# The third pooled group on VectorE, and one written order from the attention splits to the last output weights

## The chip, the cores and the metric

The kernel runs on one core of a Trainium2 chip. The metric is the device time of one launch in microseconds (us); less is better. The engines of the core run beside one another and wait for each other through semaphores: TensorE (PE in the profile; its weight loads are PEld), VectorE (DVE), ScalarE (ACT), GpSimd (POOL) and SyncE (SP), which here only issues transfers. Each engine takes its own instructions strictly in the order in which they stand.

## The reference

One layer of a streaming encoder for 1024 tokens of width 1024 (`D_MODEL`). The change lies in the first third, the mixer; the gated feed-forward, the embedding gate and the last norm follow unchanged. Of the columns of `z` the first 512 are pooled; the rest are queries, keys and values.

```python
h = x
hn = rmsnorm(h, norm_mix_g[i])
z = hn @ w_in[i]
u = z[..., :POOL_W]
q, k, v = jnp.split(z[..., POOL_W:], 3, axis=-1)
a = pool_mixer(u, pool_w[i], pool_b[i], pool_scale[i])
o = chunk_attention(q, k, v, rel_bias[i])
h = h + jnp.concatenate([a, o], axis=-1) @ w_out[i]
...
```

`pool_mixer` takes four groups of 128 channels with trailing windows of 2, 4, 8 and 16 tokens. For each group it forms the mean over the window, subtracts the token itself, multiplies by a 128x128 matrix of the group, adds a bias and scales:

```python
for gi, win in enumerate((2, 4, 8, 16)):
    start = jnp.maximum(t + 1 - win, 0)
    cnt = (t + 1 - start).astype(jnp.float32)
    pooled.append((cs[:, t + 1, gi] - cs[:, start, gi]) / cnt[None, :, None])
y = jnp.stack(pooled, axis=2) - ug
y = jnp.einsum('bsgc,gcd->bsgd', y, w) + b.reshape(N_POOL, POOL_GROUP)
return y.reshape(B, S, POOL_W) * scale
```

## The kernel before

Channels lie on the 128 partitions and tokens run along the free dimension, in two halves of 512. Every product keeps nearly fp32 precision: each operand is split into a high part, which ScalarE copies (`hi`, L122), and a low part, which VectorE forms as source minus `hi` (`lo`, L123), and `mm3` (L117 to L119) makes three matmuls, hi·hi, hi·lo and lo·hi. So one split is one ScalarE instruction and then one VectorE instruction, and a matmul of the second kind waits for the `lo`.

The mixer runs in units: for pairs of heads TensorE makes scores, transposed probabilities and values, and in the gaps it fills in the input projection of the next columns. The generator `rest()` holds these projections; the last four are the pooled groups, in the order 2, 3, 0, 1. When group g is projected, VectorE moves it from PSUM to the tile U (L555), and `project_u` appends the window sums of the group to the list `later`. Each group is done in four quarters of 256 tokens: for a window of 4 there are two additions with shifted operands (L568, 271 and 269 columns), a multiplication by 1/window (L580) and a subtraction (L581), and in the quarter with the first tokens two short instructions more (L578, L579), since their windows are shorter. All of it runs on GpSimd, `LATER` = 8 entries after each unit, and what is left runs after the last projection (`run_later(len(later))`).

Then comes the output projection of the first token half. Its first pass over eight column blocks takes the attention rows of `w_out`, `out_mm(d, 0, ..., attn, ...)`: 4 x 3 matmuls per block, each block in its own PSUM bank (2, 3, 4, 5, 0, 1, 6, 7 in turn). After blocks 2 to 5 of this pass it runs `mix(g)` for groups 2, 3, 0, 1: a split of the group (`yh`, `yl`, 1024 columns), six matmuls with the group's matrix into banks 6 and 7, two ScalarE evacuations with bias and scale into `a32` (L592), and splits of these into `catp`, the pooled rows of the next operand. All mixes use banks 6 and 7, so that the matmuls of one wait for the evacuations of the mix before. The second pass takes the pooled rows into the same eight banks, VectorE adds each bank to the residual H (L772), and the second token half follows, which also needs `cat_o(1)`, the split attention output of that half.

`out_weights(n, cs)` loads four pieces of `w_out` into a ring of four raw buffers (L601) and splits them (`[128, 4, 128]` pieces, 512 columns, which the profile counts as 128x512). H is loaded from `xT` into room that the attention output, U and `a32` held (L764).

The order of TensorE is written out for the whole kernel (`manual_schedule`). That of ScalarE and VectorE is written out for the units and, in a second block, up to the split of the mix matrices (`pwh`, `pwl`). What follows that block, the mixes among it, is placed by a list scheduler, with `cat_o(1)` at a raised priority. SyncE and GpSimd are placed by the scheduler throughout.

## Time and profile before

| | us |
|---|---|
| median of 3 runs | 1138.48 |
| their range | 1138.35 to 1140.33 |
| profiled execution | 1138.08 |
| its span | 1136.1 |
| TensorE busy | 1118.4 |
| VectorE busy | 858.9 |
| ScalarE busy | 586.4 |
| GpSimd busy | 183.6 |

The profiled execution is one more run, 0.40 us under the median. The span goes from its first to its last instruction; 1.98 us lie around it. In the rows a tile stands by its name: R and B are the split operands, F holds fp32 data, PS is PSUM. `out<-in` gives what an instruction writes and reads, a line number is that of the kernel shown, "idle before" is how long the engine stood still before the instruction, and the name after the arrow is what ended that. A row with x4 joins four instructions that followed on one another, and its time is that of all four.

### The profile page before, as it was taken

The numbers are of one execution on the slowest core, as the hardware profiler recorded it, in microseconds if no ns is written. First come the engines' busy times: TensorE is split into PE (matmuls) and PEld (weight loads), VectorE is DVE, ScalarE is ACT, GpSimd is POOL, SyncE is SP. The second block draws the span as 40 slices with busy tenths as digits, with TensorE's granted clock in tenths as the row PEclk, the third lists the DMA queues.
The fourth block names the chain that finished last, engine by engine and source line by source line (L and its number), as shares of the span: only waits on it lengthen the run. The fifth ranks groups of instructions, "written<-read, shape, count | busy, mean of one in ns | idle before, by whom it ended". The sixth has DMA issues, their size and how long they took to land.

```text
span 1136.1 us, 16167 instructions
## 1 busy us (share of the span) xinstructions
PE 1118.4 (98%) x5914; PEld 935.1 (82%) x5914; DVE 858.9 (76%) x1442; ACT 586.4 (52%) x1020; POOL 183.6 (16%) x230
## 2 busy tenths in 40 slices
PE   9999999999799999999999999999999999999997
PEld 7988898888688888888888888888888888888887
DVE  7566766778658888887787788777878889986845
ACT  8376766664654554444444444444444445574634
POOL 0010001088402210120112010301030102000000
PEclk9999999999999999999999999999999999999999
DMA  7111110115500154585557655765576556520003
GB/s 278 38 38 43 38 43 23 56 56 161 173 12 17 49 149 146 131 176 148 134 147 162 164 144 143 165 165 130 150 160 158 144 149 126 153 93 19 1 31 118
DMA packets 64879, 125.91 MB, mean 111 GB/s; under 512 B 7328, under 2 KB 8736, under 8 KB 64800
## 3 DMA queue, kind: packets, MB, share of 16 engines
q1 hardware_dynamic: 50688, 99.38, 27.0%
q0 software_dynamic: 13824, 25.17, 13.9%
q8 instruction: 46, 0.75, 0.3%
q10 hardware_dynamic: 288, 0.33, 0.1%
q14 instruction: 33, 0.27, 0.1%
HBM read 110.18 MB, written 14.68 MB: 110 GB/s over the span
## 4 chain that ended last, share of the span: by engine, by line
PE 90%; POOL 4%; DVE 2%; issue 2%; ACT 1%; DMA 0%; SPq 0%; POOLq 0%; DVEq 0%; ACTq 0%
PE PS L117 28%; PE PS L118 28%; PE PS L119 28%; POOL F L568 2%; PE PS L382 2%; PE PS L447 1%; PE PS L405 1%; PE PS L448 1%; POOL F L581 1%; POOL F L580 1%; DVE B L425 1%; DMA F<-in_xT 0%; DVE F L350 0%; PE PS L744 0%; ACT F L362 0%
## 5 line engine op out<-in xcount | busy, mean ns | idle before, releaser
L117 PE MATMUL PS<-R 128*128 128x512 f32 (+1 forms) x1104 | 425.4, 385 | 0.7 <-DVE F L453 0.6
L118 PE MATMUL PS<-R 128*128 128x512 f32 (+1 forms) x1104 | 422.0, 382 | 0.3 <-DVE R L227 0.3
L119 PE MATMUL PS<-R 128*128 128x512 f32 (+1 forms) x1104 | 421.6, 382 | 0.0
L117 PEld LDWEIGHTS PS<-R 128*128 128x128 f32 x1104 | 207.9, 188 | 44.6 <-issue 2.3
L118 PEld LDWEIGHTS PS<-R 128*128 128x128 f32 x1104 | 207.8, 188 | 41.1 <-DVE R L227 1.4
L119 PEld LDWEIGHTS PS<-R 128*128 128x128 f32 x1104 | 207.6, 188 | 40.3
L122 ACT ACTIVATE R<-F 128x512 fp32r<-128x512 f32 (+2 forms) x221 | 137.7, 637 | 181.0 <-PE PS L118 84.4
L123 DVE TENSOR_TENSOR R<-F,R 128x512 fp32r<-128x512 f32 (+2 forms) x221 | 160.1, 740 | 41.3 <-ACT R L122 38.8
L1135 DVE TENSOR_TENSOR F<-F,PS 128x512 f32<-128x512 f32 x140 | 92.8, 682 | 6.2 <-PE PS L119 6.0
L122 ACT ACTIVATE BQ<-RW 128x512 fp32r<-128x512 f32 x90 | 52.6, 623 | 82.0 <-PE PS L118 78.0
L825 DVE TENSOR_TENSOR F<-F 128x512 f32<-128x512 f32 x88 | 61.8, 702 | 42.5 <-DMA F<-in_w_up 41.6
L1078 POOL DMA_DIRECT2D RW<-Yd x56 | 49.6, 887 | 257.9 <-DMA RW<-Yd 200.8
L1078 POOL DMA_DIRECT2D RW<-in_w_down x40 | 36.1, 943 | 234.4 <-DMA RW<-in_w_down 192.2
L123 DVE TENSOR_TENSOR BQ<-RW,BQ 128x512 fp32r<-128x512 f32 x90 | 59.2, 687 | 2.9 <-PE PS L118 2.1
L118 PE MATMUL PS<-BQ 128*128 128x512 f32 x140 | 54.6, 390 | 0.1
L117 PE MATMUL PS<-R,BQ 128*128 128x512 f32 x140 | 54.5, 389 | 0.0
L119 PE MATMUL PS<-BQ 128*128 128x512 f32 x140 | 54.5, 389 | 0.0
L119 PE MATMUL PS<-R,BQ 128*128 128x512 f32 x140 | 54.5, 389 | 0.0
L117 PE MATMUL PS<-BQ 128*128 128x512 f32 x140 | 54.5, 389 | 0.0
L118 PE MATMUL PS<-R,BQ 128*128 128x512 f32 x140 | 54.5, 389 | 0.0
L362 ACT ACTIVATE F<-F,small 128x640 f32<-128x640 f32 (+4 forms) x64 | 44.0, 688 | 15.2 <-DVE small L350 13.5
L961 ACT ACTIVATE F<-F,vec 128x1024 f32<-128x1024 f32 (+1 forms) x25 | 28.6, 1143 | 43.6 <-DVE F L936 37.5
(177 smaller groups left out, 1726.2 us busy)
## 6 DMA issues: line engine op xcount, KB each, us to landing
F<-in_w_up SPq DMA_DIRECT2D x91, 256.0 KB, 3.9
RW<-Yd SPq DMA_DIRECT2D x60, 256.0 KB, 3.7
RW<-Yd POOLq DMA_DIRECT2D x56, 256.0 KB, 5.3
RW<-in_w_down SPq DMA_DIRECT2D x50, 256.0 KB, 2.9
RW<-in_w_down POOLq DMA_DIRECT2D x40, 256.0 KB, 6.0
Yd<-F SPq DMA_DIRECT2D x40, 256.0 KB, 3.7
F<-in_w_in SPq DMA_DIRECT2D x10, 512.0 KB, 3.5
F<-in_xT SPq DMA_DIRECT2D x16, 256.0 KB, 5.8
```

Source lines behind the costliest of these rows:

```text
L117: pe.matmul(ps, ahi, bhi, start=first, stop=False, skip_group_check=more)
L118: pe.matmul(ps, ahi, blo, start=False, stop=False, skip_group_check=more)
L119: pe.matmul(ps, alo, bhi, start=False, stop=last, skip_group_check=more)
L122: both = (act.activation(hi, src, AF.Copy), dve.tensor_tensor(lo, src, rv(hi), ALU.subtract))
L123: dve.tensor_tensor(lo, src, rv(hi), ALU.subtract))
L362: push(1.9 + 0.85 * z, lambda S=S, s_=s_: act.activation(S, S, AF.Exp, bias=s_[:, 0:1], scale=-1.0, accum_out=s_[:, 1:2]))
L382: pe.matmul(PS[:, places[x][y], 0:wide], q[halves[x], t * P:(t + 1) * P], k[halves[x], ki + y * wide:ki + (y + 1) * wide], start=i == 0, s ...
L568: pool.tensor_tensor(d, x, y, ALU.add))
L825: return dve.tensor_tensor(rawu[to], rawu[a], rawu[b], op)
L961: act.activation(y, Gb[:, 2 + a:2 + b], AF.Identity, bias=vec[:, C_CB + fi:C_CB + fi + 1], scale=cw(2))
L1078: pool.dma_start(t, src, accum_op=ALU.add)
L1135: dve.tensor_tensor(t, t, PS[:, 4 + d], ALU.subtract if n in (1, 5) else ALU.add)
```

## The change

Group 1, which is projected last, has its window sums on VectorE. They go to a list of their own, `tail`, and use two buffers of their own, `temps`. Multiplication and subtraction are one instruction there (`scalar_tensor_tensor`, L586 of the changed kernel), so that a quarter has three instructions in place of four, 14 for the group in place of 18.

The written order of ScalarE and VectorE reaches further: the second `manual_schedule` block now ends after the splits of the pooled output weights and `cat_o(1)`. The split of a pooled group is a function of its own, `pooled_split`, and stands apart from `mix`; the operand buffers `ya` are laid out per group. In `mix` both evacuations come ahead of both splits, and `mix(3)` calls `pooled_split(1)` in between. `run_later(len(later))` is called ahead of the block.

```diff
+        temps = [f(57.5, 272), f(58.5625, 272)]
...
-        later = []
+        later, tail = [], []
...
-            Ta, Tb = T1, T2
+            Ta, Tb = (T1, T2) if g != 1 else temps
+            eng, queue = (pool, later) if g != 1 else (dve, tail)
             for q in (3, 2, 1, 0):
...
-                    later.append(lambda d=dst[:, lo_:n], x=src[:, lo_:n], y=src[:, lo_ - m:n - m]:
-                                 pool.tensor_tensor(d, x, y, ALU.add))
+                    queue.append(lambda d=dst[:, lo_:n], x=src[:, lo_:n], y=src[:, lo_ - m:n - m]:
+                                 eng.tensor_tensor(d, x, y, ALU.add))
...
-        def pool_out(g, q, u, src):
+                queue.append(lambda q=q, u=u, src=src: pool_out(g, q, u, src, eng))
+
+        def pool_out(g, q, u, src, eng):
...
-            pool.tensor_tensor(src[:, f0:n], src[:, f0:n], cnt[:, win - 1:win].to_broadcast([P, n - f0]), ALU.mult)
-            pool.tensor_tensor(u[:, f0:n], src[:, f0:n], u[:, f0:n], ALU.subtract)
-
-        def mix(g):
-            yh, yl = ya[g % 2]
+                eng.tensor_tensor(src[:, HIST:f0], src[:, HIST:f0], cnt[:, 0:win], ALU.mult)
+                eng.tensor_tensor(u[:, HIST:f0], src[:, HIST:f0], u[:, HIST:f0], ALU.subtract)
+            if eng is pool:
+                eng.tensor_tensor(src[:, f0:n], src[:, f0:n], cnt[:, win - 1:win].to_broadcast([P, n - f0]), ALU.mult)
+                eng.tensor_tensor(u[:, f0:n], src[:, f0:n], u[:, f0:n], ALU.subtract)
+            else:
+                eng.scalar_tensor_tensor(u[:, f0:n], src[:, f0:n], 1.0 / win, u[:, f0:n], ALU.mult, ALU.subtract)
+
+        def pooled_split(g):
+            split(U[:, g, HIST:], *ya[g])
+
+        def mix(g, between=None):
+            yh, yl = ya[g]
             a32 = a32s[g % 2]
-            split(U[:, g, HIST:], yh, yl)
             for h in range(2):
...
                 act.activation(a32[:, hs], ps, AF.Identity, bias=pbs[:, g:g + 1],
                                scale=vec[:, C_PS + g:C_PS + g + 1])
+            if between:
+                between()
+            for h in range(2):
+                hs = slice(h * 512, (h + 1) * 512)
                 split(a32[:, hs], catp[h][:, g, 0], catp[h][:, g, 1])
...
-        ya = [(r(144 + 8 * s, 1024), r(148 + 8 * s, 1024)) for s in range(2)]
+        ya = {g: (r(b, 1024), r(b + 4, 1024)) for g, b in ((2, 144), (3, 152), (0, 136), (1, 144))}
...
+        run_later(len(later))
         with tc.manual_schedule(engines={mybir.EngineType.Activation, mybir.EngineType.DVE}):
             out_weights(1, attn)
             cat_o(0)
+            pooled_split(2)
             for _ in fill:
                 flush()
             flush()
             split(pw, pwh, pwl)
-        run_later(len(later))
-        with tc.high_priority(AHEAD):
+            pooled_split(3)
+            out_weights(0, attn)
+            for fn in tail[:6]:
+                fn()
+            pooled_split(0)
+            for fn in tail[6:]:
+                fn()
+            for z, d in enumerate(first_d):
+                out_mm(d, 0, first_b[z], attn, True, False)
+                if 1 <= z <= 4:
+                    mix((2, 3, 0, 1)[z - 1], (lambda: pooled_split(1)) if z == 2 else None)
+            out_weights(1, pooled)
+            out_weights(0, pooled)
             cat_o(1)
...
-        out_weights(0, attn)
-        first_b = (2, 3, 4, 5, 0, 1, 6, 7)
-        for z, d in enumerate(first_d):
-            out_mm(d, 0, first_b[z], attn, True, False)
-            if 1 <= z <= 4:
-                mix((2, 3, 0, 1)[z - 1])
         for d in first_d:
             sp.dma_start(H[d], xT[d])
-        out_weights(1, pooled)
-        out_weights(0, pooled)
```

The order of TensorE's instructions is the same before and after. On GpSimd the 18 instructions of group 1 are gone and the rest stands as it was. The other three engines differ at the following places.

VectorE from the last projection to the first residual addition. Before, L555 is the evacuation of the last projection, `B<-F,B` with 1024 columns the `lo` of a pooled group, `R<-F,R` with 4x128 a piece of `w_out`, and with 512 a piece of the attention output or of a mix:

```order
L555 TENSOR_TENSOR F<-PS,F 128x512
L123 TENSOR_TENSOR B<-F,B 128x512
L123 TENSOR_TENSOR R<-F,R 128x4x128 x4
L123 TENSOR_TENSOR B<-F,B 128x1024
L123 TENSOR_TENSOR R<-F,R 128x4x128 x2
L123 TENSOR_TENSOR R<-F,R 128x512
L123 TENSOR_TENSOR B<-F,B 128x1024
L123 TENSOR_TENSOR R<-F,R 128x512
L123 TENSOR_TENSOR R<-F,R 128x4x128
```

After, the end of the window sums of group 1 (the first rows; three quarters of three instructions each and the `lo` of group 0 stand ahead of them) and what follows on it:

```order
L570 TENSOR_TENSOR F<-F 128x271
L570 TENSOR_TENSOR F<-F 128x269
L580 TENSOR_TENSOR F<-F,small 128x4
L581 TENSOR_TENSOR F<-F 128x4
L586 SCALAR_TENSOR_TENSOR F<-F 128x252
L123 TENSOR_TENSOR R<-F,R 128x512 x2
L123 TENSOR_TENSOR B<-F,B 128x1024
L123 TENSOR_TENSOR R<-F,R 128x512 x6
L123 TENSOR_TENSOR R<-F,R 128x4x128 x8
L123 TENSOR_TENSOR R<-F,R 128x512 x4
```

Before, the pooled pieces of `w_out` (4x128) stand scattered between the mixes; after, all eight follow the last mix, and the four pieces of `cat_o(1)` (the last row), which stood ahead of the last projection's evacuation, close the block.

ScalarE at the mixes, before (L592 is an evacuation of a mix, the rows with L122 are `hi` copies):

```order
L122 ACTIVATE R<-F 128x4x128 x5
L592 ACTIVATE F<-PS,small,vec 128x512
L122 ACTIVATE R<-F 128x4x128
L122 ACTIVATE R<-F 128x512
L592 ACTIVATE F<-PS,small,vec 128x512
L122 ACTIVATE B<-F 128x1024
L122 ACTIVATE R<-F 128x512
L122 ACTIVATE R<-F 128x4x128
```

and after, where L599 is that evacuation:

```order
L122 ACTIVATE R<-F 128x4x128 x4
L122 ACTIVATE B<-F 128x1024
L599 ACTIVATE F<-PS,small,vec 128x512 x2
L122 ACTIVATE R<-F 128x512 x2
L599 ACTIVATE F<-PS,small,vec 128x512 x2
L122 ACTIVATE B<-F 128x1024
L122 ACTIVATE R<-F 128x512 x2
L599 ACTIVATE F<-PS,small,vec 128x512 x2
```

The fifth piece of weights, the first of the pooled rows, no longer stands ahead of the first evacuation, and the `hi` of group 1 (the last row with 1024 columns) stands between the evacuations of `mix(3)` and its splits.

SyncE's transfers, before (`in_w_out` are the output weights, `in_xT` the residual, `in_w_up` the first weights of the feed-forward):

```order
L764 DMA F<-in_xT 128x1024 x4
L601 DMA F<-in_w_out 128x512 x6
L764 DMA F<-in_xT 128x1024
L601 DMA F<-in_w_out 128x512
L821 DMA F<-in_w_up 128x512 x2
L601 DMA F<-in_w_out 128x512
L764 DMA F<-in_xT 128x1024
L821 DMA F<-in_w_up 128x512 x4
L764 DMA F<-in_xT 128x1024
```

and after (L783, L612 and L838 are the same three):

```order
L783 DMA F<-in_xT 128x1024
L612 DMA F<-in_w_out 128x512 x4
L838 DMA F<-in_w_up 128x512 x2
L783 DMA F<-in_xT 128x1024 x2
L612 DMA F<-in_w_out 128x512 x4
L838 DMA F<-in_w_up 128x512 x4
L783 DMA F<-in_xT 128x1024 x4
```

Four of the residual's loads, those of blocks 4 to 7, moved from the front to the end, behind all output weights and six loads for the feed-forward: their room is that of the attention output, which `cat_o(1)` now reads last.

More of the change, by code (lines that the diff above doesn't have):

```diff
@@ L566, in project_u @@
                     lo_ += m
-                    later.append(lambda d=dst[:, lo_:n], x=src[:, lo_:n], y=src[:, lo_ - m:n - m]:
-                                 pool.tensor_tensor(d, x, y, ALU.add))
+                    queue.append(lambda d=dst[:, lo_:n], x=src[:, lo_:n], y=src[:, lo_ - m:n - m]:
+                                 eng.tensor_tensor(d, x, y, ALU.add))
                     src, dst = dst, (Tb if dst is Ta else Ta)
                     m *= 2
-                later.append(lambda q=q, u=u, src=src: pool_out(g, q, u, src))
-        def pool_out(g, q, u, src):
+                queue.append(lambda q=q, u=u, src=src: pool_out(g, q, u, src, eng))
+        def pool_out(g, q, u, src, eng):
             win, n, f0 = WINDOWS[g], HIST + 256, HIST
@@ L577, in pool_out @@
                 f0 = HIST + win
-                pool.tensor_tensor(src[:, HIST:f0], src[:, HIST:f0], cnt[:, 0:win], ALU.mult)
-                pool.tensor_tensor(u[:, HIST:f0], src[:, HIST:f0], u[:, HIST:f0], ALU.subtract)
-            pool.tensor_tensor(src[:, f0:n], src[:, f0:n], cnt[:, win - 1:win].to_broadcast([P, n - f0]), ALU.mult)
-            pool.tensor_tensor(u[:, f0:n], src[:, f0:n], u[:, f0:n], ALU.subtract)
-        def mix(g):
-            yh, yl = ya[g % 2]
+                eng.tensor_tensor(src[:, HIST:f0], src[:, HIST:f0], cnt[:, 0:win], ALU.mult)
[9 more added lines that the diff above has]
+            yh, yl = ya[g]
             a32 = a32s[g % 2]
-            split(U[:, g, HIST:], yh, yl)
             for h in range(2):
@@ L696, in cat_o @@
                 split(o32[:, c, h * 512:(h + 1) * 512], cato[h][:, c, 0], cato[h][:, c, 1])
+        first_d = (4, 5, 6, 7, 0, 1, 2, 3)
+        first_b = (2, 3, 4, 5, 0, 1, 6, 7)
+        run_later(len(later))
         with tc.manual_schedule(engines={mybir.EngineType.Activation, mybir.EngineType.DVE}):
@@ L754, in rows @@
                     act.activation(dst, self.out, AF.Copy)
-        first_d = (4, 5, 6, 7, 0, 1, 2, 3)
-        out_weights(0, attn)
-        first_b = (2, 3, 4, 5, 0, 1, 6, 7)
-        for z, d in enumerate(first_d):
-            out_mm(d, 0, first_b[z], attn, True, False)
-            if 1 <= z <= 4:
-                mix((2, 3, 0, 1)[z - 1])
         for d in first_d:
             sp.dma_start(H[d], xT[d])
-        out_weights(1, pooled)
-        out_weights(0, pooled)
         tc.keep_in_program_order(act.activation(small[:, 2:3], mhalf, AF.Gelu))
```

## The prediction

> **What bounds the kernel now.** I read the page first, then the busy time by stage, then TensorE's own rows and waits where the stage has a hole.

> ```profile
> PE 1118.4 (98%) x5914; PEld 935.1 (82%) x5914; DVE 858.9 (76%) x1442; ACT 586.4 (52%) x1020; POOL 183.6 (16%) x230
> PE 90%; POOL 4%; DVE 2%; issue 2%; ACT 1%; DMA 0%; SPq 0%; POOLq 0%; DVEq 0%; ACTq 0%
> 0.00:263.00 263.00, 258.66 (x2016) 221.66 (x2017) 176.50 (x415) 171.77 (x347) 48.26 (x84) 1.00 0.21 69
> 263.00:310.50 47.50, 41.24 (x179) 32.54 (x178) 37.84 (x42) 27.78 (x46) 30.65 (x35) 0.96 0.59 186
> 310.50:1136.00 825.50, 818.52 (x3723) 680.88 (x3722) 644.52 (x985) 386.85 (x627) 104.70 (x112) 1.00 0.47 120
> ```

> The stage rows give length, then busy time of PE, PEld, DVE, ACT and POOL, granted clock, DMA share. TensorE is the bound everywhere; 47.5 us around the mixes hold 6.3 us of its idle time and a clock of 0.96. GpSimd's 4% of the chain lie there too. TensorE's order does not change, so a gain can only be its waits and its slow clock there.

> ```profile
> 273.99 0.39 PE L117 MATMUL PS<-R 128*128 128x512 f32 x1
> 285.17 0.50 PE L117 MATMUL PS<-B 128*128 128x512 f32 x1 [1.10 <-ACT F L592]
> 285.93 0.50 PE L118 MATMUL PS<-B 128*128 128x512 f32 x1 [0.26 <-DVE B L123]
> 287.04 0.50 PE L117 MATMUL PS<-B 128*128 128x512 f32 x1 [0.37 <-ACT F L592]
> 299.39 0.80 PE L117 MATMUL PS<-B 128*128 128x512 f32 x1 [4.52 <-ACT F L592]
> 302.81 0.39 PE L119 MATMUL PS<-R 128*128 128x512 f32 x1
> 310.56 0.39 PE L117 MATMUL PS<-R 128*128 128x512 f32 x1
> 295.00:300.00 5.00, 0.60 (x2) 0.51 (x3) 1.81 (x2) 2.90 (x5) 1.99 (x5) 0.92 0.18 68
> 300.00:305.00 5.00, 5.00 (x18) 3.98 (x17) 4.29 (x8) 4.98 (x10) 0.00 (x0) 0.74 0.67 224
> ```

> At 273.99 the first attention pass of the output projection begins, at 310.56 the pooled pass. Between them stand 8 x 12 matmuls and four mixes of 6, 120 in all. From 302.81 to 310.56 there are 34 starts in 7.75 us, 0.228 each; 120 would take 27.4 us and they take 36.57. So **9.2 us** are lost: about 2.3 around `mix(3)` (285 to 287), 4.7 ahead of `mix(1)`, and most of the rest after it, where the clock fell for a while ((0.08 + 0.26) x 5 = 1.7 us).

> Why TensorE waits:

> ```profile
> 283.82 0.63 ACT L122 ACTIVATE R<-F 128x512 fp32r<-128x512 f32 x1 [7.92 <-DMA F<-in_w_out]
> 284.36 0.76 ACT L592 ACTIVATE F<-PS,small,vec 128x512 f32<-128x512 f32 x1
> 276.42 1.18 POOL L581 TENSOR_TENSOR F<-F 128x254 f32<-128x254 f32 x1
> 279.61 0.95 POOL L568 TENSOR_TENSOR F<-F 128x271 f32<-128x271 f32 x1 [2.00 <-DVE F L555]
> 296.36 0.71 POOL L581 TENSOR_TENSOR F<-F 128x252 f32<-128x252 f32 x1
> ACT B L122 <- POOL F L581: 5.7, 1, 5.7
> 277.04 0.69 DVE L555 TENSOR_TENSOR F<-PS,F 128x512 f32<-128x512 f32 x1
> 279.98 4.24 DVE L123 TENSOR_TENSOR R<-F,R 128x512 fp32r<-128x512 f32 x4
> 284.14 1.74 DVE L123 TENSOR_TENSOR B<-F,B 128x1024 fp32r<-128x1024 f32 x1
> 298.19 1.22 DVE L123 TENSOR_TENSOR B<-F,B 128x1024 fp32r<-128x1024 f32 x1 [3.27 <-ACT B L122]
> 300.56 3.10 DVE L123 TENSOR_TENSOR R<-F,R 128x512 fp32r<-128x512 f32 x5 [0.55 <-ACT R L122]
> ```

> First, ScalarE stood 7.9 us at a piece of the pooled weights that had not landed, with the first evacuation of `mix(2)` queued behind it; `mix(3)` waited for that bank. Second, GpSimd began group 1 at 279.61 and ended at 297.07; ScalarE's split of the group stood 5.7 us for it, and `mix(1)` with it. The last rows show what both engines cost each other: a `lo` of 512 columns takes 1.06 us while GpSimd runs (4.24 for four) and 0.62 when it rests (3.10 for five); one of 1024 takes 1.74 against 1.22.

> **The change, part by part.** *Group 1 on GpSimd* goes: 17.5 us from 279.61 to 297.07, and with it VectorE's slow rate after group 0 ends at 277.60.

> *Group 1 on VectorE.* No row shows it; the nearest are

> ```profile
> 1114.73 0.43 DVE L1285 TENSOR_TENSOR F<-V,F 128x256 f32<-128x256 f32 x1 [0.88 <-ACT F L1284]
> 1115.19 0.42 DVE L1286 TENSOR_TENSOR F<-F 128x256 f32<-128x256 f32 x1
> L978 DVE SCALAR_TENSOR_TENSOR F<-F,V 128x512 f32<-128x512 f32 x20 | 13.8, 688 | 0.0
> L1286 DVE TENSOR_TENSOR F<-F 128x512 f32<-128x512 f32 x13 | 8.9, 689 | 0.2
> L617 DVE TENSOR_TENSOR small<-vec 128x4 f32<-128x4 f32 x1 | 0.2, 164 | 1.8 <-DMA vec<-in_vecs 1.8
> ```

> Two additions of 256 columns, the second needing the first, start 0.46 apart; 15 columns more make 0.47. The fused form costs as much as an addition (688 against 689 at 512), so 0.46. Eight additions, four fused, two short ones of 0.20: 3.76 + 1.84 + 0.40 = **6.0 us**. The upper bound is the rate beside GpSimd, 1.06, so 14.8; the lower the bare durations, 5.5. I take 6.0, since GpSimd is idle by then.

> [...]

> *Is that in time for `mix(1)`?* TensorE's 273.99 rests on `cat_o(0)`, which moves ahead there, so I keep it. With no waits TensorE reaches `mix(1)` after 78 matmuls, at 291.8, its second half at 292.5. VectorE's written order:

> ```profile
> 264.48 0.63 ACT L122 ACTIVATE R<-F 128x512 fp32r<-128x512 f32 x1 [3.66 <-DMA F<-in_w_out]
> 268.60 0.85 DVE L453 TENSOR_TENSOR F<-PS,F 64x256 f32<-64x256 f32 x2
> L592 ACT ACTIVATE F<-PS,small,vec 128x512 f32<-128x512 f32 x8 | 5.9, 765 | 0.0
> L122 ACT ACTIVATE B<-F 128x1024 fp32r<-128x1024 f32 x4 | 4.2, 1047 | 5.7 <-POOL F L581 5.7
> 266.87 4.28 ACT L122 ACTIVATE R<-F 128x512 fp32r<-128x512 f32 x8
> ```

> - The first `lo` can start when its `hi` ends, 265.1. Eight splits beside GpSimd 8.5, two value additions 0.85, the `lo` of group 2 1.66, some 0.3 for the second weight piece to land: 276.4.
> - Two evacuations and the mix matrices, 3 x 0.61: 278.2. Group 3, 1.14: 279.4 (`mix(3)` needs it at 283.6). Four attention weights, 2.4: 281.8 (needed at 289.0).
> - Six steps of the chain 2.8, the `lo` of group 0 1.14, eight steps 3.2: 289.0. Two splits of `mix(2)` 1.2, the `lo` of group 1 1.2: 291.4, just ahead of 291.8.

> ScalarE stands at the `hi` of group 1 until 289.0, and queued behind it are the splits of `mix(3)` and the evacuations of `mix(0)`, for which `mix(1)` waits: 1.0 + 2 x 0.53 (4.28 for eight) + 0.77 = 2.8, so bank 6 is free at 291.8 and bank 7 at 292.4. Both paths end within 0.4 us of TensorE. From here each us that the chain is late costs TensorE a us. I allow **0.3 us** for hops between engines.

> *Pooled weights after the last mix.* ScalarE no longer stands at their transfers with an evacuation behind it, which removes the waits at `mix(3)`. The first four now end near 299.3: `mix(1)` ends at 293.2, its evacuations, splits and four `hi` take 1.5 + 1.1 + 2.1, and VectorE trails by one piece. Needed at 301.4; hidden with 2 us. The second four wait for their ring slots, land some 3 us after, and are split near 304; needed four blocks later, at 312.3.

> *`cat_o(1)` last.* It ends on VectorE near 307; nobody needs it before the second token half, 8 x 12 matmuls after 301.4, at 323.2. Early on, three `hi` copies of 0.6 us leave ScalarE between 161 and 215, where TensorE hardly waits (4.3 us idle in the 263 of the first stage row): 0 to 0.9 us, taken as nothing.

> *SyncE.* The loads of H for blocks 4 to 7 go past the pooled weights and six feed-forward loads, and wait for `cat_o(1)`:

> ```profile
> 273.81 2.95 SPq L764 DMA_DIRECT2D F<-in_xT  x4
> DMA to landing us min/median/max: 3.4/3.9/5.7
> 313.48 0.69 DVE L772 TENSOR_TENSOR F<-F,PS 128x512 f32<-128x512 f32 x1 [4.26 <-PE PS L119]
> ```

> Issued from about 305 to 307 instead of 273.8 to 276.8, with 3.4 to 5.7 to land, they come between 309 and 313. VectorE's first residual addition, at 313.48 before, could start at 304.1 and waits for them then, with the other additions queued behind it. TensorE only notices at 323.2, when it takes the first bank again: cover of some 9 us, and no cost.

> *Sum.* 9.2 - 0.3 = 8.9 us. Against the profiled execution, 1138.08 - 8.9 = 1129.2; the median of the runs lies 0.4 higher, so **1129.6 us**. With the whole 9.2 and the 0.9 of the early copies, 1128.4.

> **The rivals.** *The mixes wait for VectorE in part (1131 to 1134).* If the two engines shut each other out for whole instructions, each split beside GpSimd would take its own 0.69 and all of a GpSimd addition, 0.64 alone:

> ```profile
> 264.28 0.64 POOL L568 TENSOR_TENSOR F<-F 128x271 f32<-128x271 f32 x1
> ```

> That is 1.33 in place of 1.06; eight of them make the chain 2.2 us late, and `mix(1)` with it: 1131.8. For it: the slow rows are real. Against: four took 4.24, not 5.3. [...] Any other delay of VectorE counts alike; steps of 0.7 in place of 0.46 would cost 3.4, so 1133.0. And a wait as long as the old one would bring the slow clock back, 1.7 us more.

> *No change.* ScalarE, whose order is now fixed, passes the stall on: if the chain ended at 297 as GpSimd did, `mix(1)` would start at 299.8, and all would be as before, 1138. It would need steps of 1.0 us on an engine without a neighbour; the rows speak against it.

> *Slower: the residual's loads.* If H for blocks 4 to 7 landed so late that VectorE's additions did not free the first bank by 323.2, TensorE would stand at the second half. The last load may land up to 321 or so, 14 us after its issue; from there each us costs one, and past 23 us the gain is gone: landing after 28 us gives 1143. For it: the loads share the queues with six of the feed-forward. Against: the longest took 5.7, four in a burst.

> **How the numbers follow.** A difference under 0.2%, 2.3 us, can't be told from none here. Forecast (1128 to 1131) 0.70; in part late (1131 to 1136) 0.20; no change 0.05; slower 0.05. So faster 0.90, same 0.05, slower 0.05. The range 1128.0 to 1133.5 takes in the forecast, splits of 1.33 and steps of 0.7, and leaves out under 2 in 10.

> **What would show it.** Right: from the first attention matmul to the first pooled one some 27.5 us; no wait above 0.5 us at a mix; granted clock 1.00 throughout; window sums on VectorE at 0.42 to 0.46 a step; splits of 512 at 0.6 from group 0's end; VectorE's first residual addition waiting for the transfer of `xT` with no wait of TensorE behind it. Wrong: a wait of TensorE for L599 at `mix(1)`, a ScalarE wait for VectorE above 3 us at the `hi` of group 1 with TensorE idle, or TensorE waiting for VectorE's additions where the second half begins.

## The result and the profile after

| | before | after |
|---|---|---|
| median of the runs, us (lowest to highest) | 1138.81 (1138.35 to 1140.33) | 1129.46 (1128.78 to 1130.02) |
| the profiled execution, us / its span | 1138.08 / 1136.1 | 1130.02 / 1128.3 |
| the 120 matmuls from the first attention matmul to the first pooled one, us | 36.57 | 27.20 |

The ratio after to before is 0.9915, with a 95% interval of 0.9898 to 0.9933. Faster by 0.85%, and 0.1 us from the forecast of 1129.6.

The page after, its busy line and its chain of waits, GpSimd's share of which has gone:

```profile
PE 1115.4 (99%) x5914; PEld 934.0 (83%) x5914; DVE 855.7 (76%) x1456; ACT 586.3 (52%) x1020; POOL 166.3 (15%) x212
PE 94%; DVE 2%; issue 1%; ACT 1%; DMA 0%; SPq 0%; POOL 0%; POOLq 0%; DVEq 0%; ACTq 0%
```

Busy time by stage, in the columns of the prediction, cut at the new start of the pooled pass:

```profile
0.00:263.00 263.00, 258.50 (x2016) 221.38 (x2016) 176.56 (x415) 169.89 (x344) 48.30 (x84) 1.00 0.21 68
263.00:301.50 38.50, 38.50 (x181) 32.25 (x180) 30.98 (x48) 24.74 (x41) 13.17 (x17) 1.00 0.47 148
301.50:1128.00 826.50, 818.44 (x3722) 680.36 (x3720) 648.18 (x994) 391.68 (x636) 104.82 (x112) 1.00 0.48 124
```

The middle stage went from 47.5 us to 38.5; TensorE is busy in all of it, at a granted clock of 1.00. The stage behind is 1.0 us longer, for a reason that the last two rows of the next view show.

The timeline of the changed kernel around the mixes (start, duration, engine, line; xN for neighbours in one row), TensorE first, then ScalarE, GpSimd, VectorE and SyncE, and at the end two rows of TensorE from a later stage:

```profile
274.02 0.39 PE L117 MATMUL PS<-R 128*128 128x512 f32 x1
291.70 0.39 PE L117 MATMUL PS<-B 128*128 128x512 f32 x1
301.23 0.39 PE L117 MATMUL PS<-R 128*128 128x512 f32 x1
280.35 1.46 ACT L599 ACTIVATE F<-PS,small,vec 128x512 f32<-128x512 f32 x2 [2.30 <-PE PS L119]
287.66 1.07 ACT L122 ACTIVATE B<-F 128x1024 fp32r<-128x1024 f32 x1 [1.78 <-DVE F L586]
274.52 1.58 POOL L583 TENSOR_TENSOR F<-F,small 128x254 f32<-128x254 f32 x1
276.22 0.74 POOL L584 TENSOR_TENSOR F<-F 128x254 f32<-128x254 f32 x1
268.15 6.34 DVE L123 TENSOR_TENSOR R<-F,R 128x512 fp32r<-128x512 f32 x6
274.42 1.21 DVE L123 TENSOR_TENSOR B<-F,B 128x1024 fp32r<-128x1024 f32 x1
278.60 2.49 DVE L123 TENSOR_TENSOR R<-F,R 128x512 fp32r<-128x512 f32 x4
281.01 0.91 DVE L570 TENSOR_TENSOR F<-F 128x271 f32<-128x271 f32 x2
281.95 0.42 DVE L586 SCALAR_TENSOR_TENSOR F<-F 128x256 f32<-128x256 f32 x1
282.29 0.91 DVE L570 TENSOR_TENSOR F<-F 128x271 f32<-128x271 f32 x2
287.22 0.41 DVE L586 SCALAR_TENSOR_TENSOR F<-F 128x252 f32<-128x252 f32 x1
288.76 1.23 DVE L123 TENSOR_TENSOR B<-F,B 128x1024 fp32r<-128x1024 f32 x1
310.05 0.69 DVE L789 TENSOR_TENSOR F<-F,PS 128x512 f32<-128x512 f32 x1 [0.96 <-DMA F<-in_xT]
325.73 0.69 DVE L764 TENSOR_TENSOR F<-F 128x512 f32<-128x512 f32 x1
279.31 2.13 SPq L612 DMA_DIRECT2D F<-in_w_out  x4
304.59 2.31 SPq L783 DMA_DIRECT2D F<-in_xT  x4
692.28 0.50 PE L117 MATMUL PS<-R 128*128 128x512 f32 x1 [0.81 <-ACT F L929]
728.81 0.50 PE L119 MATMUL PS<-R 128*128 128x512 f32 x1 [0.41 <-DVE R L123]
```

From 274.02 to 301.23 TensorE never waits; 291.70 is the start of `mix(1)`. ScalarE evacuates `mix(2)` as soon as TensorE gives it up, and stands 1.8 us, not 5.7, for group 1. GpSimd ends group 0 at 276.96 and rests from there. VectorE's chain for group 1 runs from 281.01 to 287.63 with the `lo` of group 0 in it, and the `lo` of group 1 ends at 289.99.

By the 120 matmuls 9.4 us are gained, by the spans of the two profiled executions 7.9. The rest is in the last two rows: at 692 and 729 us this execution waits where the one before hardly did. The stretch with both places (1700 matmuls) lasts between 385.6 and 387.3 us over the profiled executions of all the kernels of this study, 385.7 before and 387.3 after. It does not follow the edits made at 260 to 330 us, so the experiments are read from the 120 matmuls first, and from the medians second.

### The profile page after: what moved, and what is told of

It is laid out like the page before. It is cut to its first block, busy times and chain, and to the rows that moved or that the text cites. A ratio compares the mean times of both kernels' runs of the same rounds, so it can differ in the third digit from the quotient of the medians.

```text
span 1128.3 us, 16160 instructions
## 1 busy us (share of the span) xinstructions
PE 1115.4 (99%) x5914; PEld 934.0 (83%) x5914; DVE 855.7 (76%) x1456; ACT 586.3 (52%) x1020; POOL 166.3 (15%) x212
## 4 chain that ended last, share of the span: by engine, by line
PE 94%; DVE 2%; issue 1%; ACT 1%; DMA 0%; SPq 0%; POOL 0%; POOLq 0%; DVEq 0%; ACTq 0%
PE PS L117 29%; PE PS L118 29%; PE PS L119 29%; PE PS L383 2%; PE PS L448 2%; PE PS L449 2%; PE PS L406 1%; DVE B L426 1%; DMA F<-in_xT 0%; DVE F L351 0%; PE PS L770 0%; ACT F L363 0%; ACT F L451 0%; DVE F L361 0%; DVE BQ L123 0%
## 5 line engine op out<-in xcount | busy, mean ns | idle before, releaser
L117 PE MATMUL PS<-R 128*128 128x512 f32 (+1 forms) x1104 | 424.7, 385 | 1.6 <-ACT F L929 0.8
L119 PE MATMUL PS<-R 128*128 128x512 f32 (+1 forms) x1104 | 421.5, 382 | 0.4 <-DVE R L123 0.4
L118 PE MATMUL PS<-R 128*128 128x512 f32 (+1 forms) x1104 | 421.6, 382 | 0.3 <-DVE R L228 0.3
L117 PEld LDWEIGHTS PS<-R 128*128 128x128 f32 x1104 | 207.5, 188 | 45.4 <-issue 2.4
L119 PEld LDWEIGHTS PS<-R 128*128 128x128 f32 x1104 | 207.5, 188 | 41.3 <-DVE R L123 0.8
L118 PEld LDWEIGHTS PS<-R 128*128 128x128 f32 x1104 | 207.6, 188 | 40.2 <-DVE R L228 1.6
L122 ACT ACTIVATE R<-F 128x512 fp32r<-128x512 f32 (+2 forms) x221 | 137.3, 636 | 168.6 <-PE PS L118 83.0
L123 DVE TENSOR_TENSOR R<-F,R 128x512 fp32r<-128x512 f32 (+2 forms) x221 | 154.1, 713 | 40.7 <-ACT R L122 40.1
L122 ACT ACTIVATE BQ<-RW 128x512 fp32r<-128x512 f32 x90 | 52.6, 622 | 75.5 <-PE PS L118 71.6
L123 DVE TENSOR_TENSOR BQ<-RW,BQ 128x512 fp32r<-128x512 f32 x90 | 59.1, 685 | 2.1 <-PE PS L118 1.3
L118 PE MATMUL PS<-BQ 128*128 128x512 f32 x140 | 54.6, 390 | 0.1
L978 ACT ACTIVATE F<-F,vec 128x1024 f32<-128x1024 f32 (+1 forms) x25 | 28.6, 1143 | 50.2 <-DVE F L953 44.0
L119 PE MATMUL PS<-BQ 128*128 128x512 f32 x140 | 54.5, 389 | 0.0
L118 PE MATMUL PS<-R,BQ 128*128 128x512 f32 x140 | 54.5, 389 | 0.0
L119 PE MATMUL PS<-R,BQ 128*128 128x512 f32 x140 | 54.5, 389 | 0.0
L117 PE MATMUL PS<-R,BQ 128*128 128x512 f32 x140 | 54.5, 389 | 0.0
L117 PE MATMUL PS<-BQ 128*128 128x512 f32 x140 | 54.5, 389 | 0.0
```

The source lines that it names most:

```text
L117: pe.matmul(ps, ahi, bhi, start=first, stop=False, skip_group_check=more)
L118: pe.matmul(ps, ahi, blo, start=False, stop=False, skip_group_check=more)
L119: pe.matmul(ps, alo, bhi, start=False, stop=last, skip_group_check=more)
L122: both = (act.activation(hi, src, AF.Copy), dve.tensor_tensor(lo, src, rv(hi), ALU.subtract))
L123: dve.tensor_tensor(lo, src, rv(hi), ALU.subtract))
L978: act.activation(y, Gb[:, 2 + a:2 + b], AF.Identity, bias=vec[:, C_CB + fi:C_CB + fi + 1], scale=cw(2))
```

## The experiments

Theory: the 9.2 us had two causes, GpSimd's late group 1 and ScalarE's order of a late weight piece ahead of an evacuation; the change removes each with one of its parts. Rivals: one part does all; or VectorE's new order merely hides a wait which has room to come back.

The ratios are to the kernel before, run beside them (medians of 1138.1 and 1138.2).

| kernel | the 120 matmuls, us | median, us (lowest to highest) | ratio to before, 95% |
|---|---|---|---|
| order alone | 33.74 | 1134.77 (1134.13 to 1135.96) | 0.9973 (0.9964 to 0.9982) |
| order alone, split later | 33.77 | 1134.32 (1133.60 to 1134.96) | 0.9966 (0.9956 to 0.9976) |
| VectorE alone | 29.86 | 1131.84 (1131.09 to 1132.44) | 0.9949 (0.9930 to 0.9968) |
| 8 more steps | 31.78 | 1132.96 (1131.06 to 1134.67) | 0.9955 (0.9939 to 0.9970) |
| 16 more steps | 36.45 | 1137.46 (1136.66 to 1138.58) | 0.9994 (0.9984 to 1.0003) |
| GpSimd beside the chain | 32.88 | 1134.17 (1133.00 to 1134.86) | 0.9965 (0.9953 to 0.9977) |
| piece first | 27.20 | 1128.94 (1128.60 to 1129.02) | 0.9918 (0.9902 to 0.9934) |
| piece late | 28.57 | 1129.69 (1129.14 to 1130.26) | 0.9923 (0.9909 to 0.9938) |
| piece first and late | 29.35 | 1131.21 (1130.17 to 1133.36) | 0.9943 (0.9926 to 0.9960) |
| second half's splits early | 29.49 | 1130.92 (1130.45 to 1131.35) | 0.9941 (0.9922 to 0.9959) |
| second half's splits late | 27.20 | 1135.52 (1134.78 to 1137.05) | 0.9979 (0.9970 to 0.9989) |
| no second load of w_v | 27.20 | 1128.20 (1127.84 to 1128.88) | 0.9911 (0.9896 to 0.9926) |

**Each part alone.** The order alone: the changed kernel with group 1 back on GpSimd.

```
-            Ta, Tb = (T1, T2) if g != 1 else temps
-            eng, queue = (pool, later) if g != 1 else (dve, tail)
+            Ta, Tb = T1, T2
+            eng, queue = pool, later
...
             flush()
+            run_later(len(later))
             split(pw, pwh, pwl)
```

> Group 1 is back on GpSimd, the written order of the changed kernel stays. Theory (both halves are needed; ScalarE, now in a fixed order, stands at the high part of group 1 with the evacuations of mix(0) behind it): GpSimd starts the group at 277 and ends near 294.5; 1.0 for the high part, 1.1 for the splits of mix(3) and 0.8 for the first evacuation give a free bank at 297.4, so that TensorE waits 5.7 us at mix(1) and some 1.9 more go to a slow clock: 1129.5 + 7.6 = 1137 us, between 1135 and 1139. Rival (the written order brings the gain, the engine of group 1 matters little): 1130 to 1132 us.

The same with the split of group 1 called in `mix(0)` instead of `mix(3)`:

```
-                    mix((2, 3, 0, 1)[z - 1], (lambda: pooled_split(1)) if z == 2 else None)
+                    mix((2, 3, 0, 1)[z - 1], (lambda: pooled_split(1)) if z == 3 else None)
```

> As the run before, but the split of group 1 is called in mix(0) and not in mix(3), so that it stands behind the evacuations of mix(0). Theory: the banks are free, mix(1) waits for GpSimd alone: high part at 295.5, low part at 296.8, TensorE loses 4.9 us and some 1.7 by the clock: 1136 us, between 1134 and 1138, some 1 us under the run before. Rival: no difference between the two, both at 1130 to 1132.

VectorE alone: the kernel before, with the diff's lines on `temps`, `tail`, `eng` and `pool_out`, and

```
         run_later(len(later))
+        for fn in tail:
+            fn()
         with tc.high_priority(AHEAD):
```

> The kernel before with the window sums of group 1 on VectorE and nothing else; the scheduler still places ScalarE and VectorE. Theory: the wait ahead of mix(1) shrinks, since the group is done near 292, its low part near 295, to about 1 to 1.5 us with no slow clock; the 2.3 us around mix(3) stay, since the first pooled piece of weights still stands ahead of the evacuation of mix(2) and still lands near 283.5. 1138.6 - 5.7 = 1133 us, between 1131.5 and 1134.5. Rival (the engine of group 1 is the whole gain): 1129.5 to 1130.5.

The order alone, timeline of TensorE at `mix(1)` and of GpSimd in group 1, then a window in the columns of the stage rows:

```profile
295.47 0.79 PE L117 MATMUL PS<-B 128*128 128x512 f32 x1 [3.80 <-ACT F L599]
277.02 2.53 POOL L570 TENSOR_TENSOR F<-F 128x271 f32<-128x271 f32 x2
285.33 1.08 POOL L570 TENSOR_TENSOR F<-F 128x271 f32<-128x271 f32 x1
287.63 0.64 POOL L570 TENSOR_TENSOR F<-F 128x269 f32<-128x269 f32 x1
291.91 0.71 POOL L584 TENSOR_TENSOR F<-F 128x252 f32<-128x252 f32 x1
295.00:300.00 5.00, 4.53 (x11) 3.57 (x12) 2.71 (x5) 4.46 (x8) 0.00 (x0) 0.50 0.35 97
```

VectorE alone, timeline of TensorE at `mix(3)` and of ScalarE:

```profile
284.41 0.51 PE L117 MATMUL PS<-B 128*128 128x512 f32 x1 [0.69 <-ACT F L597]
285.08 0.50 PE L118 MATMUL PS<-B 128*128 128x512 f32 x1 [0.16 <-DVE B L123]
286.27 0.50 PE L117 MATMUL PS<-B 128*128 128x512 f32 x1 [0.46 <-ACT F L597]
283.06 0.63 ACT L122 ACTIVATE R<-F 128x512 fp32r<-128x512 f32 x1 [7.24 <-DMA F<-in_w_out]
```

The order takes away the waits at `mix(3)` and leaves one at `mix(1)`; VectorE takes that away and leaves the 2.3 us at `mix(3)`. Each removes one cause: 36.57 - 33.74 = 2.8 and 36.57 - 29.86 = 6.7, together 9.5 against the 9.4 of both. The order alone came out 2 us better than I expected, just below the range given: GpSimd ended group 1 at 292.62, not 294.5, since from 287 on, with VectorE resting, its additions took 0.64 us in place of 1.08. Where the split is called hardly mattered, though I had expected 1 us of it: the 120 matmuls take the same time in both forms, which wait for the same end, the later one in two pieces (2.8 and 1.0 us). VectorE alone was expected to keep a wait of 1 to 1.5 us ahead of `mix(1)`; none stayed there (0.1 us), and its median lies low in the range given.

**How much room the chain has.** Steps that change no value, behind the chain on VectorE: 8, and 16.

```
+            slow = U[:, 1, HIST:HIST + 271]
+            for _ in range(8):
+                dve.tensor_tensor(slow, slow, slow, ALU.max)
             for z, d in enumerate(first_d):
```

> Eight more steps of 271 columns on VectorE behind the chain of group 1, which change no value: 8 x 0.46 = 3.7 us later for everything that VectorE does after the chain. Theory (the two last banks of mix(1) come free about 1.3 us before TensorE asks for them in the changed kernel, and from there on each microsecond of the chain is one of the span): TensorE waits about 2.4 us at mix(1), about 1132 us (1131 to 1133). Rival (the chain has more room than that, since ScalarE and not VectorE ends the wait): 1129.5 to 1130.3 us.

> Sixteen such steps: 7.4 us later. Theory (slack 1.3 us, then one for one, and a wait of some 6 us is followed by a stretch at half the clock, as the waits of about 4 us were): 6.1 us of wait and 1.7 to 2.6 us of slow matmuls, about 1137.5 us (1136 to 1139). Rival (one for one without the slow stretch): 1135.5 us.

Timelines of VectorE and of TensorE at `mix(1)`, and windows with the granted clock; 8 steps:

```profile
287.38 3.77 DVE L729 TENSOR_TENSOR F<-F 128x271 f32<-128x271 f32 x8
294.00 0.50 PE L117 MATMUL PS<-B 128*128 128x512 f32 x1 [2.65 <-ACT F L599]
295.00:300.00 5.00, 5.00 (x16) 3.92 (x16) 3.75 (x7) 5.00 (x10) 0.00 (x0) 0.66 0.51 150
```

and 16 steps:

```profile
287.65 7.57 DVE L729 TENSOR_TENSOR F<-F 128x271 f32<-128x271 f32 x16
298.07 0.80 PE L117 MATMUL PS<-B 128*128 128x512 f32 x1 [6.42 <-ACT F L599]
295.00:300.00 5.00, 1.93 (x5) 1.55 (x6) 4.54 (x8) 4.71 (x8) 0.00 (x0) 0.66 0.15 52
300.00:305.00 5.00, 5.00 (x16) 3.96 (x15) 3.17 (x6) 4.43 (x8) 0.00 (x0) 0.65 0.38 114
```

TensorE starts `mix(1)` 2.8 and 6.6 us after its turn (294.00 and 298.07 against 291.19 and 291.49, one matmul behind the last), so the room was 3.77 - 2.8 = 7.57 - 6.6 = 1.0 us, and past it the cost is one for one, as the theory had it with 1.3. What it lacked is the slow clock after a wait of only 2.65 us: matmuls started 0.43 us apart in place of 0.23 (the granted clock is the 0.66 of the window), another 1.8 us (4.6 more for the 120 matmuls, less the 2.8). Sixteen steps give the whole gain back: 36.45 us against 36.57 before the change.

**What GpSimd costs VectorE.** Additions on GpSimd, on two arrays that nobody else uses then:

```
+        for _ in range(14):
+            pool.tensor_tensor(T1[:, 16:272], T2[:, 16:272], T2[:, 16:272], ALU.add)
         with tc.manual_schedule(engines={mybir.EngineType.Activation, mybir.EngineType.DVE}):
```

> Fourteen additions of 256 columns on GpSimd, on two arrays of its own, beside the chain of group 1 on VectorE. Theory (GpSimd and VectorE slow each other down by a part, as in the splits of 512 columns that took 1.06 instead of 0.62 us): the steps of the chain grow from 0.45 to 0.7 to 0.8 us, the chain ends 3 to 5 us later, TensorE waits 2 to 4 us at mix(1): 1131.5 to 1133.5 us. Rival (one of the two holds the memory for a whole instruction): each step takes its own 0.45 us and one of GpSimd's 0.6 to 0.7 us, so 1.05 to 1.15 us, the chain ends 8 us later, TensorE waits 6 to 7 us: 1136 to 1139 us.

Timeline of this kernel: GpSimd and VectorE at a split, then GpSimd, VectorE and GpSimd in the chain, then two steps of VectorE when GpSimd has ended:

```profile
279.11 0.94 POOL L713 TENSOR_TENSOR F<-F 128x256 f32<-128x256 f32 x1
279.50 1.10 DVE L123 TENSOR_TENSOR R<-F,R 128x512 fp32r<-128x512 f32 x1
283.19 0.69 POOL L713 TENSOR_TENSOR F<-F 128x256 f32<-128x256 f32 x1
283.44 0.74 DVE L570 TENSOR_TENSOR F<-F 128x269 f32<-128x269 f32 x1
283.96 0.69 POOL L713 TENSOR_TENSOR F<-F 128x256 f32<-128x256 f32 x1
290.69 0.91 DVE L570 TENSOR_TENSOR F<-F 128x271 f32<-128x271 f32 x2
```

In the chain the two engines take turns, step for step, 0.77 us a pair (283.19 to 283.96). The price is the one I expected, 0.7 to 0.8 us a step; the mechanism is the rival's. VectorE's step ends at 284.18, 0.30 us behind the end of GpSimd's addition at 283.88; GpSimd's next ends at 284.65, 0.47 behind that of VectorE. The split ends at 280.60, 0.55 behind GpSimd's addition at 280.05. So each engine waits until the other has ended, rather than running at a lower rate beside it: in the traces of before and after, the 35 splits of 512 columns that began while GpSimd was at a computation and were lengthened (24 and 11) all end between 0.545 and 0.553 us behind its instruction. (Five more lost nothing: one in each trace met an instruction of GpSimd 2.9 us long, and three began in the last 0.13 us of one.) Alone a step takes 0.44 us and a split 0.68, in both cases 0.14 more than the 0.30 and 0.55. That much of an instruction, and of GpSimd's about as much (0.64 alone against 0.47), passes while the other engine is still at work. The rival charged both lone times in full, 0.46 + 0.64 = 1.10 us a pair, where 0.30 + 0.47 is what they cost; so its 1136 us and more did not come. TensorE lost 2.4 us at `mix(1)`, as expected, but also 1.5 at `mix(0)`, for which the `lo` of group 0 came late, and 1.7 by the slow clock (granted 0.66 from 295 to 300 us); that is why the median lies above the range given.

**The late weight piece.** The first pooled piece goes back ahead of the evacuation of `mix(2)`; a second kernel keeps the change's order and has the buffers of the weights freed 2.35 us later; a third has both edits.

```
             for fn in tail[6:]:
                 fn()
+            out_weights(1, pooled[0:1])
...
-            out_weights(1, pooled)
+            out_weights(1, pooled[1:4])
```

> Only the split of the first pooled piece of the output weights goes back ahead of the evacuation of mix(2); the other three pieces stay where the change has them. Theory (the piece lands about 282.2 us, so ScalarE stands for about 2 us less than the 7.9 us of before, in which the loads were also issued later): TensorE waits 0 to 0.7 us at mix(3): 1129.5 to 1130.2 us, so the order of the evacuation and the later loads each carried a part of the 2.3 us. Rival (the order on ScalarE alone makes the whole of it): 2.3 us, 1131.7 us.

```
             pooled_split(3)
+            late = U[:, 1, HIST:HIST + 271]
+            for _ in range(5):
+                dve.tensor_tensor(late, late, late, ALU.max)
             out_weights(0, attn)
```

> Five steps of 271 columns (2.35 us) on VectorE ahead of its splits of the four attention weights, which change no value, with the changed kernel's order kept. The buffers of the pooled weights then come free 2.35 us later and their first piece lands about 283.8 us, as in the kernel before, but ScalarE evacuates mix(2) ahead of it. Theory (the stall needs both, a late piece and the evacuation queued behind it): no wait at mix(3), and 1.4 us at mix(1), because the chain is late by 2.35 us and had some 0.9 of room in the runs with more steps: 1130.9 us (1130 to 1131.7). Rival (VectorE's lateness alone makes the stall at mix(3)): about 2 us there, 1131.5 us or more.

> The same five steps, and the first pooled piece split ahead of the evacuation of mix(2), as before the change. Theory: the piece lands about 283.8 us, its split ends 284.4, the evacuation 285.1, where TensorE asks at 283.1: a wait of about 2 us at mix(3) is back, and the one at mix(1) is small, since TensorE now comes 2 us later itself: 1131.5 us (1130.8 to 1132.5). Rival (the loss at mix(3) in the kernel before came from GpSimd's use of the memory, not from this order): none at mix(3), 1.4 us at mix(1), as in the run without the early piece.

Timelines: piece first, ScalarE;

```profile
281.45 0.63 ACT L122 ACTIVATE R<-F 128x512 fp32r<-128x512 f32 x1 [3.92 <-DMA F<-in_w_out]
281.99 1.43 ACT L599 ACTIVATE F<-PS,small,vec 128x512 f32<-128x512 f32 x2
```

piece late, SyncE and TensorE;

```profile
281.70 2.14 SPq L612 DMA_DIRECT2D F<-in_w_out  x4
292.87 0.50 PE L117 MATMUL PS<-B 128*128 128x512 f32 x1 [1.06 <-ACT F L599]
```

piece first and late, ScalarE and TensorE:

```profile
283.70 0.63 ACT L122 ACTIVATE R<-F 128x512 fp32r<-128x512 f32 x1 [6.16 <-DMA F<-in_w_out]
284.24 1.43 ACT L599 ACTIVATE F<-PS,small,vec 128x512 f32<-128x512 f32 x2
285.05 0.50 PE L117 MATMUL PS<-B 128*128 128x512 f32 x1 [1.85 <-ACT F L599]
```

With the early piece the old order costs nothing at all (27.20), though narrowly: the first evacuation ends at 282.75, and TensorE takes its bank at 283.04. With the new order the late piece costs nothing at `mix(3)`; only both together bring the wait there back, 2.1 us. I had expected each to carry a part; it is an "and". The 1.4 us at `mix(1)` in the second kernel is again 2.35 less 1.0 of room. The medians of the first two kernels lie 0.6 and 0.3 us below the ranges given; the second's 1.4 us shows in the 120 matmuls and only as 0.2 us in the medians, whose single runs differ by about 1 us. What makes the piece early is VectorE: SyncE issues the load when VectorE has split an attention weight out of the same buffer, at 279.31 in the changed kernel and 281.70 here.

**The second token half's splits.** `cat_o(1)` right behind `cat_o(0)`; and, in another kernel, 18 steps ahead of it where the change has it.

```
             cat_o(0)
+            cat_o(1)
             pooled_split(2)
...
             out_weights(0, pooled)
-            cat_o(1)
```

> The changed kernel with the split of the second half's attention output, four pieces, right behind that of the first half instead of at the end; the residual's loads can then start some 27 us earlier. Theory (VectorE's chain has little slack, the residual's loads have much): VectorE is 3.4 us later from there on, the mix matrices are ready near 281 (1 us of wait in mix(2)), the chain of group 1 ends near 291 and mix(1) waits 1.2 more: 1131.7 us, between 1130.5 and 1133. Rival (the late loads of the residual cost something): equal to the changed kernel or faster, 1128 to 1129.5 us.

```
             out_weights(0, pooled)
+            for _ in range(18):
+                dve.tensor_tensor(T1[:, 16:272], T1[:, 16:272], T1[:, 16:272], ALU.max)
             cat_o(1)
```

> Eighteen steps of 256 columns on VectorE ahead of the splits of the second token half of the attention outputs, which change no value: those splits, and the loads of the residual into the same memory, come about 8 us later (loads issued 313 to 315 us, landing 317 to 322). Theory (cover of some 9 us): TensorE waits 0 to 1 us where its second half begins, 1129.5 to 1130.5 us. Rival (the cover is smaller, and the additions that free the first bank come too late): 3 to 8 us there, 1132.5 to 1137.5 us.

Early, timeline of TensorE at `mix(2)` and `mix(1)`:

```profile
280.64 0.50 PE L119 MATMUL PS<-B 128*128 128x512 f32 x1 [0.89 <-DVE B L123]
293.52 0.50 PE L117 MATMUL PS<-B 128*128 128x512 f32 x1 [0.80 <-ACT F L599]
```

Late, timeline of VectorE and TensorE:

```profile
332.21 0.68 DVE L766 TENSOR_TENSOR F<-F 128x512 f32<-128x512 f32 x1
333.04 1.84 PE L772 MATMUL PS<-small,F 128*128 128x1 f32 x8 [4.86 <-DVE F L766]
```

Early came out as expected: VectorE has no time for four more splits there. Late did not: my theory said at most 1 us. At the first bank of the second token half TensorE indeed did not wait, but the sums of the first norm (L772 here, L770 in the changed kernel) come soon after. They need all eight residual additions and the norm's seven additions behind them; the last of those ended at 326.42 in the changed kernel, where TensorE asked at 328.43: 2.0 us of room. Here it ended at 332.89, 6.5 us later, TensorE stood 4.9 us, and the half clock (granted 0.60 from 330 to 335 us, 0.71 from 335 to 340) took most of the other 2.8 by which the 408 matmuls behind the mixes grew (96.67 us against 88.98).

**Work nobody reads.** The changed kernel without the second load and split of the value weights:

```
-                    if (h, k) == (0, 2):
+                    if (h, k) == (0, 2) and ct != blocks_[-1]:
```

> The changed kernel without the second load and split of the value weights, which nobody reads. Theory (TensorE waits for nothing around them): no gain, 1129.5 us (1128.8 to 1130). Rival (VectorE's and ScalarE's time there is on the path): 0.5 to 2 us faster, 1127.5 to 1129 us.

The median is 1.3 us lower, 0.1%, below the range that I gave for no gain and inside that of the rival, and the intervals of the two ratios overlap nearly whole. The profile does not place it at the edit, which lies ahead of the mixes: the first attention matmul starts at 273.59 (274.02 in the changed kernel, 273.52 with the piece first), the 120 matmuls take 27.20, and most of the difference between the two profiled executions lies at the two late waits of the changed kernel. A gain is not shown, and a small one is not excluded.

## Why the prediction was right, and where it was not

- *9.2 us lost, 0.3 to be kept.* Right: 9.37 went, no wait stayed. That the median came within 0.1 us is luck: the gain was 0.5 larger than forecast, and the median before, 1138.81 with a fourth run, 0.3 higher than the 1138.48 that the forecast started from.
- *GpSimd's late group as the greater cause, the weight piece as the smaller.* Right in size, 6.7 and 2.8 us apart. In "removes the waits at `mix(3)`" the order on ScalarE was given the whole credit; the runs show that the order or the earlier load would each have been enough. The second I had not counted as an effect of the change.
- *The chain at 0.46 to 0.47 a step, 6.0 us.* 5.4 us, 0.1 below the lower bound. Additions kept 0.47 (281.01 to 281.95 for two), but a step that does not read the result of the fused one before it starts 0.34 behind it (281.95 to 282.29). Bounds taken from dependent pairs were no bounds for that.
- *VectorE's schedule, no room at `mix(1)`.* The order of events was right, each some tenths early: weights 0.7, chain 0.7 more, the `lo` of group 1 at 289.99 for 291.4. So 1.0 us of room where I had none. "From here each us that the chain is late costs TensorE a us" holds past that, and the half clock comes on top.
- *Splits of 1.06 beside GpSimd.* Right (6.34 for six); the `lo` of 1024 columns at 274.42 took 1.21, not the 1.66 of the sum: there GpSimd waited for VectorE.
- *Pooled weights and `cat_o(1)`.* Right: the first four were ready near 298.3 (299.3 forecast; its own terms, 293.2 + 4.7 and one piece of 0.6, add up to 298.5), all eight near 304, `cat_o(1)` at 306.4 (307).
- *SyncE, "TensorE only notices at 323.2 ... cover of some 9 us".* The loads were issued when forecast (304.59), took 5.3 to 7.2 us to land where 3.4 to 5.7 were reckoned with (the first addition, at 310.05, waited for its own), and cost nothing. But the step is wrong: the consumer that decides is the first norm's sums at 328.43, with 2.0 us of room. The slower rival was thus far nearer than its price of "14 us after its issue"; the forecast held because the change used up less than it had, and that was luck, since this room had not been reckoned.
- *The rival of exclusive sharing.* Its mechanism holds, its price does not. "Four took 4.24, not 5.3" was held against it; but what counts for a split is 0.55 us, and for GpSimd's instruction 0.47 to 0.60, and not the lone 0.69 and 0.64. That gives the 1.06 that the forecast took from the row, so the forecast did not depend on the mechanism. The other prices of lateness were right in kind and left out how early the slow clock sets in.

## What to carry to other kernels

A stall with two conditions, a late transfer and work queued behind its reader, vanishes when either goes; test the conditions together before crediting one edit. When work is moved later, walk every reader down to the first that TensorE itself waits for, reductions over all the blocks included, not only the next bank. When VectorE and GpSimd run at once as here, on fp32 operands in arrays of their own, reckon with their instructions one behind the other, less the first 0.14 us or so of each (0.77 us a pair here, of 0.44 and 0.64 alone). And near the edge a wait on TensorE can cost more than its length: 2.65 us cost 4.6 here.

## What the hardware showed

The slow clock is not proportional to the wait. The table has five of the executions that had such a stretch, with the granted clock of the windows of 5 us that hold it. It was 0.50 in the one window that lay in such a stretch whole, and from that follows the time at half clock (0.66 is 0.34 x 2 x 5 = 3.4 us):

| kernel | wait, us | granted clock | half clock, us |
|---|---|---|---|
| before | 4.5 | 0.92, 0.74 from 295 us | 3.4 |
| order alone | 3.8 | 0.89, 0.50, 0.93 from 290 us | 6.8 |
| 8 more steps | 2.65 | 0.66 from 295 us | 3.4 |
| 16 more steps | 6.42 | 0.66, 0.65 from 295 us | 6.9 |
| second half's splits late | 4.86 | 0.60, 0.71 from 330 us | 6.9 |

VectorE's 0.34 us from the start of a fused step of 256 columns to the next independent step is shorter than that step itself, 0.42; a dependent pair of additions stays at 0.47 for 271 columns (281.01 to 281.95 for two).

And the cost of sharing is not even; in these rows it falls on whoever comes second: the 1.21 us split at 274.42 lost nothing beside GpSimd, whose instruction of 254 columns at 274.52 took 1.58 us and ended 0.47 behind the split (276.10 and 275.63), while in the six splits ahead of it (6.34 us) VectorE came second and lost 0.4 us each.
